# Shift and scale of the first norm: from split to plain fp32 products in two column tiles of TensorE

## Chip, cores and metric

One core of a Trainium2 chip runs one layer of a backbone on 256 latent and 256 context tokens of width 2048, in fp32. The metric is the device time of one execution in microseconds.

## The reference, cut to what matters

For the latent tokens and for the context tokens (with `c_ctx` in place of `c`) the layer begins with

```python
mod = silu(c) @ ada_w + ada_b          # (2048) @ (2048, 12288): six sections of 2048 columns
h   = rmsnorm(x) * (1 + scale1) + shift1   # section 0 is the shift, section 1 the scale
z   = h @ w_in                         # (2048, 3680)
```

Attention, spatial gating, a gated linear attention, an output projection and a mixture of 16 experts follow. Of `ada_w`, sections 0 and 1 (2 x 16.8 MB) are needed before the first projection; the other four belong to later places.

## The kernel before, in words

**Stages.** `phase1` computes the first norm and the in-projection. Behind it come the mixers, the output projection, the second norm, routing, and the expert stage, which streams 403 MB of weights.

**The first norm.** `rows` loads x and ctx (8 loads of 512 KB on SP) and takes their sums of squares on ACT; `scale` multiplies the rows. `ada1(f0, nf)` makes shift and scale for `nf` blocks ("columns") of 128 model dimensions from block `f0` on, for both token kinds at once. The units are (0, 2), (2, 2), (4, 4), (8, 4), (12, 4). A unit has three parts: `load` steps, `copies` and `cols`, and one `hcol` for each column.

- `load(sec, k0)` brings 4 blocks of 128 rows of `ada_w` for one section into a `raw` buffer (pool of 6, shared with the loads of `w_in`), in 512 KB loads by SP (L169). A unit of two columns is loaded in pieces of 1 KB, one of four in pieces of 2 KB. ACT rounds the buffer to fp32r (`hi`, L129), DVE forms the rest (`lo`, L130), each in a pool of two buffers. TensorE multiplies both (L347) with a weight tile of four columns (`c4`: the rounded value and the rest of silu(c) and of silu(c_ctx)). Only section 0 of the first unit goes unsplit, as plain fp32 products (L342).
- `copies` brings the sums from PSUM to SBUF on ACT (L356). `cols` transposes them on TensorE (L365) and adds the parts and the bias on DVE (L368 to L372).
- `hcol(j)` transposes one column of x and ctx (4 transposes into a `psB` bank, L384, two such banks), applies scale and shift on ACT (L388, two halves), and splits the result into `hT` (L129 on ACT, L130 on DVE).

**The in-projection.** `w_in_steps(k0, k1, chunk)` streams `w_in` by chunks of columns: a load into `raw`, the split (three buffers each), and three fp32r products (L425) for each 128 tokens and 128 rows. `hT` has four quarters of four columns. In a first round all nine chunks are multiplied with the first quarter alone (`win`, k 0 to 4), woven with the later units of `ada1`; when the norm is complete, a second round (`w1`, `w2`, `w3`) takes quarters two to four and adds.

**What sets the order.** Program order, woven by `merge` and `weave`, is the priority by which a scheduler orders each engine's instructions ahead of time; every engine then works strictly in that order. SP issues nearly all loads, so a load that waits for its buffer holds all loads behind it.

```python
units = [self.ada1(*u) for u in ((0, 2), (2, 2), (4, 4), (8, 4), (12, 4))]
...
for l, p, h in units[2:]:
    rest += merge(l, late) + p
    late = h
weave(win[1:], rest + late)
```

Of the kernel before, what the change touches and what calls it, by code (L numbers as in the profile page):

```python
# [18 lines left out]
D = 2048  # L19
KT = 16  # L20
# [4 lines left out]
KQ = KT // NQ  # L25
# [73 lines left out]
class Kern:  # L99
# [112 lines left out]
    def phase1(self):  # L212
        nc, tc, T = self.nc, self.tc, self.T
# [8 lines left out]
        with ExitStack() as ph, ExitStack() as p1:  # L222
# [4 lines left out]
            self.adap = [p1.enter_context(self.pool(name=n, bufs=2, side="right")) for n in ("ahi", "alo")]  # L227
# [40 lines left out]
            self.c4 = self.cp.tile([128, KT, 2, 2], F32R, name="c4")  # L268
            scv = self.sc.rearrange("p (v k) -> p k v", v=2)
            nc.scalar.activation(self.c4[:, :, :, 0], scv, AF.Copy)  # L270
            nc.vector.tensor_tensor(self.c4[:, :, :, 1], scv, self.c4[:, :, :, 0], op=OP.subtract)
# [21 lines left out]
            units = [self.ada1(*u) for u in ((0, 2), (2, 2), (4, 4), (8, 4), (12, 4))]  # L293
# [3 lines left out]
            win = [f for c in chunks for f in self.w_in_steps(0, 4, c)]  # L297
            for f in [rows(i) for i in range(4)] + l0[:2] + [scale(0)] + l0[2:] + p0 + h0 + win[:1] + l1 + p1_ + h1 + [scale(1)]:
                f()
# [21 lines left out]
    def ada1(self, f0, nf):  # L321

        nc = self.nc
        T = self.T
        st = {}
        cw = nf * 128
        q, j0 = divmod(f0, KQ)

        whole = (f0 == 0, False)
        rows = [2 if w else 4 for w in whole]  # L330
        scv = self.sc.rearrange("p (v k) -> p k v", v=2)

        def load(sec, k0):
            def f():
                if k0 == 0:
                    st[sec] = self.C()
                c0 = sec * D + f0 * 128
                if whole[sec]:
                    raw = self.rawp.tile([128, 4, cw], F32, name="raw", tag="raw")
                    nc.sync.dma_start(raw, T["ada_w"][0, k0 * 128:(k0 + 4) * 128, c0:c0 + cw].rearrange("(k p) c -> p k c", p=128))  # L340
                    for k in range(4):
                        nc.tensor.matmul(st[sec][:2, :cw], scv[:, k0 + k], raw[:, k], start=(k0 + k == 0), stop=(k0 + k == KT - 1))  # L342
                    return
                h, l = self.stream(T["ada_w"][0], c0, c0 + cw, k0, 4, self.adap)
                for part, w in enumerate((h, l)):
                    for k in range(4):
                        nc.tensor.matmul(st[sec][:4, :cw], self.c4[:, k0 + k].rearrange("p a b -> p (a b)"),  # L347
                                         w[k], start=(k0 + k == 0 and part == 0),
                                         stop=(k0 + k == KT - 1 and part == 1))
            return f  # L350

        def copies():
            s4 = self.maccp.tile([128, 1024], F32, name="macc", tag="macc")
            st["s4"] = [s4[:rows[i], i * cw:(i + 1) * cw] for i in range(2)]
            for sec in range(2):
                nc.scalar.activation(st["s4"][sec], st[sec][:rows[sec], :cw], AF.Copy)  # L356

        def cols():
            cps = self.B()
            md = self.sp.tile([128, 2, KQ, 2], F32, name="md", bufs=2)[:, :, :nf]  # L360
            for sec in range(2):
                n = rows[sec]
                for j in range(nf):
                    o = sec * 16 + j * n
                    nc.tensor.transpose(cps[:, o:o + n], st["s4"][sec][:, j * 128:(j + 1) * 128], self.ident[:n, :n])  # L365
                cv = cps[:, sec * 16:sec * 16 + nf * n].rearrange("p (k v a) -> p k v a", k=nf, v=2)
                b = self.col[:, 48 + 16 * sec + f0:48 + 16 * sec + f0 + nf]
                nc.vector.tensor_tensor(md[:, sec], cv[:, :, :, 0], b[:, :, None].to_broadcast([128, nf, 2]), op=OP.add)  # L368
                if not whole[sec]:
                    nc.vector.tensor_tensor(md[:, sec], md[:, sec], cv[:, :, :, 1], op=OP.add)  # L370
# [4 lines left out]
            if j0 == 0:  # L375
                h = self.h_new(q)
                self.hT[q] = (h[:, 0], h[:, 1])

        def hcol(j):
            def f():  # L380
                k = f0 + j
                tp = self.B()
# [3 lines left out]
                md = st["md"]  # L386
# [4 lines left out]
                self.split(hi[:, j0 + j], lo[:, j0 + j], full)  # L391
            return f
        out = []
# [1191 lines left out]
```

## Time and profile before

| | |
|---|---|
| three runs | 1649.9, 1656.56, 1658.26 us (median 1656.56) |
| the profiled execution | 1650.78 us, span 1649.0 us |
| TensorE products (PE) | busy 1487.6 us, 90% of the span |
| VectorE (DVE), ScalarE (ACT) | 647.5 us (39%), 447.6 us (27%) |
| HBM read | 566.73 MB, 346 GB/s over the span |

The profile is of one execution. Its span is read as stages: from about 740 us on the expert stage moves 420 to 422 GB/s in nearly every slice. The change lies in the first 165 us, where PE, DVE, ACT and DMA all have high shares, so only a view of that stretch tells what sets its time. A busy share of PE counts modelled ends, which overlap the next start; two starts give the true spacing.

### The profile page before, as it was taken

To read this page: it belongs to the slowest core of one execution; us is meant where nothing else is said; L and a number is where in the kernel's file an instruction comes from. 1 tells how busy PE (TensorE), PEld (TensorE's weight loads), DVE (VectorE), ACT (ScalarE), POOL (GpSimd) and SP (SyncE) were. 2 spreads that over 40 slices of the span, in tenths; PEclk is the share of its full clock that TensorE was granted. 3 is DMA by queue.
4 is the path that set the end of the run, shared out by engine and by line. 5 is a ranking of instruction groups with operands and counts; after the bars stand their busy time and mean duration, and the time that the engine had idled before them with its cause. 6 is when DMAs were issued, how large, how long until landed. Compare 5 with 4: busy or idle time off the path is not lost. (4 is left out here: it accounts for less than half of the span.)

```text
span 1649.0 us, 17919 instructions
## 1 busy us (share of the span) xinstructions
PE 1487.6 (90%) x6875; PEld 793.5 (48%) x6875; DVE 647.5 (39%) x1093; ACT 447.6 (27%) x870; POOL 37.7 (2%) x52
## 2 busy tenths in 40 slices
PE   4999999998899989899998988997988998988877
PEld 1566878986667758443333333333333333333322
DVE  4687788988987665311111121111021111111102
ACT  4788224257656543210011001011001001001000
POOL 0000100001000000000000000000000000000000
PEclk9999999999999999899999999999999999999999
DMA  9899987765787577689999999999999999999996
GB/s 296 262 322 318 324 284 235 239 228 159 248 290 248 195 231 305 243 324 422 421 420 421 421 420 421 421 421 421 421 420 421 419 421 421 420 421 420 422 421 243
DMA packets 140880, 570.09 MB, mean 346 GB/s; under 512 B 19195, under 2 KB 37906, under 8 KB 92662
## 3 DMA queue, kind: packets, MB, share of 16 engines
q1 hardware_dynamic: 133424, 563.93, 88.0%
q0 software_dynamic: 1696, 2.97, 0.6%
q10 hardware_dynamic: 5670, 1.99, 0.5%
q8 instruction: 56, 0.92, 0.2%
q14 instruction: 34, 0.28, 0.1%
HBM read 566.73 MB, written 4.21 MB: 346 GB/s over the span
## 5 line engine op out<-in xcount | busy, mean ns | idle before, releaser
L1295 PE MATMUL psC<-mraw,xT 128*64 128x512 f32 x2048 | 466.1, 595 | 66.0 <-DMA mraw<-in_moe_w_dram 66.0
L1295 PEld LDWEIGHTS psC<-mraw,xT 128*64 128x64 f32 x2048 | 154.6, 137 | 372.2 <-issue 245.9
L1295 PE MATMUL psA<-mraw,aT 128*64 128x512 f32 x1024 | 225.8, 597 | 0.0
L130 DVE TENSOR_TENSOR lo<-raw,hi 128x1024 fp32r<-128x1024 f32 (+3 forms) x170 | 198.3, 1182 | 64.0 <-ACT hi L129 56.6
L1385 DVE TENSOR_TENSOR act<-silu,psC 64x512 f32<-64x512 f32 x32 | 22.0, 690 | 488.5 <-ACT silu L1296 488.5
L129 ACT ACTIVATE hi<-raw 128x1024 fp32r<-128x1024 f32 (+3 forms) x170 | 171.3, 1024 | 155.9 <-DMA raw<-in_w_in_dram 57.6
L1296 ACT ACTIVATE silu<-psC 64x512 f32<-64x512 f32 x32 | 18.9, 590 | 701.0 <-PE psC L1295 701.0
L425 PE MATMUL psA<-hi,hT 128*128 128x512 f32 (+2 forms) x832 | 182.2, 346 | 5.6 <-ACT hi L129 2.3
L425 PEld LDWEIGHTS psA<-hi,hT 128*128 128x128 f32 x832 | 136.3, 190 | 28.1 <-ACT hi L129 5.8
L1295 PEld LDWEIGHTS psA<-mraw,aT 128*64 128x64 f32 x1024 | 74.2, 138 | 138.3 <-issue 134.8
L1401 DVE TENSOR_TENSOR zs<-psA,gate 128x512 f32<-128x512 f32 x64 | 44.3, 692 | 173.7 <-PE psA L1295 171.9
L425 PE MATMUL psA<-lo,hT 128*128 128x512 f32 (+2 forms) x416 | 106.0, 348 | 0.9 <-DVE lo L130 0.9
L1295 PE MATMUL psB<-Sr,x 128*128 128x256 f32 x256 | 70.6, 412 | 22.8 <-ACT xT L1296 20.9
L455 DVE SCALAR_TENSOR_TENSOR gate<-raw,sc,gate 128x1024 f32<-128x1024 f32 x64 | 81.9, 1280 | 3.9 <-DMA raw<-in_ada_w_dram 3.7
L455 DVE SCALAR_TENSOR_TENSOR macc<-raw,sc,macc 128x1024 f32<-128x1024 f32 x60 | 76.7, 1279 | 14.9 <-DMA raw<-in_ada_w_dram 14.4
L425 PEld LDWEIGHTS psA<-lo,hT 128*128 128x128 f32 x416 | 70.2, 190 | 11.1 <-issue 1.5
L1295 PEld LDWEIGHTS psB<-Sr,x 128*128 128x128 f32 x256 | 47.8, 201 | 50.3 <-ACT xT L1296 34.2
L1295 PE MATMUL psB<-zs,W 128*128 128x512 f32 x128 | 62.8, 619 | 1.7 <-DVE stage L1437 1.5
L1437 DVE TENSOR_TENSOR stage<-stage,psB 128x512 f32<-128x512 f32 x64 | 43.3, 686 | 45.5 <-PE psB L1295 44.9
L1296 ACT ACTIVATE xT<-psB,mod 128x256 f32<-128x256 f32 x64 | 36.0, 563 | 78.0 <-PE psB L1295 78.0
L347 PE MATMUL psC<-hi,c 128*4 128x512 f32 (+1 forms) x144 | 36.9, 361 | 13.4 <-ACT hi L129 12.8
L1295 PEld LDWEIGHTS psB<-zs,W 128*128 128x128 f32 x128 | 21.1, 189 | 39.1 <-DVE stage L1437 20.1
(389 smaller groups left out, 1333.9 us busy)
## 6 DMA issues: line engine op xcount, KB each, us to landing
mraw<-in_moe_w_dram SPq DMA_DIRECT2D x383, 1024.0 KB, 19.8
raw<-in_ada_w_dram SPq DMA_DIRECT2D x192, 512.0 KB, 5.0
raw<-in_w_in_dram SPq DMA_DIRECT2D x44, 512.0 KB, 5.1
raw<-in_w_out_dram SPq DMA_DIRECT2D x32, 512.0 KB, 4.7
raw<-in_w_in_dram SPq DMA_DIRECT2D x10, 432.0 KB, 5.2
raw<-in_mla_w_ukv_dram SPq DMA_DIRECT2D x8, 512.0 KB, 5.0
raw<-in_mla_w_uq_dram SPq DMA_DIRECT2D x8, 384.0 KB
xs<-in_x_dram SPq DMA_DIRECT2D x4, 512.0 KB, 4.7
```

Of the source, the lines that this page charges most:

```text
L129: self.nc.scalar.activation(hi, src, AF.Copy)
L130: self.nc.vector.tensor_tensor(lo, src, hi, op=OP.subtract)
L347: nc.tensor.matmul(st[sec][:4, :cw], self.c4[:, k0 + k].rearrange("p a b -> p (a b)"), w[k], start=(k0 + k == 0 and part == 0), stop=(k0 + ...
L425: nc.tensor.matmul(acc[t][:, :w], xw[:, j, t * 128:(t + 1) * 128], ww[:, k], start=(kk == k0 and p == 0 and k == 0), stop=(kk + n == k1 an ...
L455: i = nc.vector.scalar_tensor_tensor(a, raw, self.sc[:, k:k + 1], a, op0=OP.mult, op1=OP.add)
L1295: mm = lambda *a, **kw: tc.keep_in_program_order(nc.tensor.matmul(*a, skip_group_check=True, **kw))
L1296: act_op = lambda *a, **kw: tc.keep_in_program_order(nc.scalar.activation(*a, **kw))
L1385: TT(a[:, h * 512:(h + 1) * 512], s, st["U"][h][CAP:], op=OP.mult)
L1401: TT(st["zs"][:, s], st["Z"][j], self.gate2[:, s], op=OP.mult)
L1437: TT(s, s, p, op=OP.add)
```

## The change

`ada1` no longer splits its weights. Every product is a plain fp32 one, with a weight tile of two columns (silu(c) and silu(c_ctx)); two products stand in two column tiles of TensorE, with output partitions from 0 and from 64. In units of two and four columns the tiles hold the two sections. The last two units become one, (8, 8), which loads 128 rows of 1024 columns at a time, in pieces of 4 KB, and has two PSUM banks, one for each section, and in each the two halves in the two tiles. A `load` step now brings both sections (two loads of 512 KB) into a pool of its own, `araw`, with four buffers. The products of a step are chained, so that the tiles alternate. `c4` is gone, and `cols` has half as many rows to transpose and no parts to add. The eight `hcol` of the last unit all come behind its products. In the changed code the in-projection's line is L424, the products' L347, the loads' L339, the transposes' L368 and L386, and `hcol`'s on ACT L390.

```diff
-            self.adap = [p1.enter_context(self.pool(name=n, bufs=2, side="right")) for n in ("ahi", "alo")]
+            self.adap = p1.enter_context(self.pool(name="araw", bufs=4, side="right"))
...
-            units = [self.ada1(*u) for u in ((0, 2), (2, 2), (4, 4), (8, 4), (12, 4))]
+            units = [self.ada1(*u) for u in ((0, 2), (2, 2), (4, 4), (8, 8))]
...
-        cw = nf * 128
+        cw = min(nf * 128, 512)
+        nb = nf * 128 // cw
+        per = 1024 // (cw * nb)
...
+        place = lambda sec, b: (sec, 64 * b) if nb == 2 else (0, 64 * sec)
...
-                h, l = self.stream(T["ada_w"][0], c0, c0 + cw, k0, 4, self.adap)
-                for part, w in enumerate((h, l)):
-                    for k in range(4):
-                        nc.tensor.matmul(st[sec][:4, :cw], self.c4[:, k0 + k].rearrange("p a b -> p (a b)"),
-                                         w[k], start=(k0 + k == 0 and part == 0),
-                                         stop=(k0 + k == KT - 1 and part == 1))
+                for sec in (1, 0):
+                    raw = self.adap.tile([128, per, nb * cw], F32, name="araw", tag="araw")
+                    c0 = sec * D + f0 * 128
+                    self.last_load = nc.sync.dma_start(raw, T["ada_w"][0, k0 * 128:(k0 + per) * 128, c0:c0 + nb * cw].rearrange("(k p) c -> p k c", p=128))
+                    raws.append((sec, raw))
+                todo = [(k, sec, b, raw) for k in range(per) for sec, raw in raws[::-1] for b in range(nb)]
+                last = None
+                for k, sec, b, raw in todo:
+                    i, o = place(sec, b)
+                    with self.tc.high_priority(), self.tc.issue_after(last.ins) if last else nullcontext():
+                        last = nc.tensor.matmul(st["ps"][i][o:o + 2, :cw], scv[:, k0 + k], raw[:, k, b * cw:(b + 1) * cw],
+                                                start=(k0 + k == 0), stop=(k0 + k == KT - 1), skip_group_check=True)
...
-        for k0 in range(0, KT, 4):
-            out += [load(1, k0), load(0, k0)]
-        return out, [copies, cols], [hcol(j) for j in range(nf)]
+        return [load(k0) for k0 in range(0, KT, per)], [copies, cols], [hcol(j) for j in range(nf)]
```

Three places of the new order. First SP's loads, from the third unit to the end of shift and scale. Before:

```order
L169 DMA raw<-in_ada_w_dram 128x2x512 x4
L169 DMA raw<-in_w_in_dram 128x2x512
L169 DMA raw<-in_ada_w_dram 128x2x512 x2
L169 DMA raw<-in_w_in_dram 128x2x512
L169 DMA raw<-in_ada_w_dram 128x2x512 x4
L169 DMA raw<-in_w_in_dram 128x2x512
L169 DMA raw<-in_ada_w_dram 128x2x512 x2
```

and now:

```order
L339 DMA araw<-in_ada_w_dram 128x2x512 x8
L169 DMA raw<-in_w_in_dram 128x288
L339 DMA araw<-in_ada_w_dram 128x2x512 x6
L169 DMA raw<-in_w_in_dram 128x2x512
L339 DMA araw<-in_ada_w_dram 128x2x512 x2
L169 DMA raw<-in_w_in_dram 128x2x512 x2
L339 DMA araw<-in_ada_w_dram 128x1024 x32
L169 DMA raw<-in_w_in_dram 128x2x512 x3
```

The `w_in` loads of this stretch moved ahead of the large unit, whose 32 loads follow one another.

Second, TensorE's products in the middle of the large units. Before (`c` is the split weight tile, two records of `hi` and `lo` for each load half):

```order
L347 MATMUL psC<-hi,c_157 4x512 x4
L347 MATMUL psC<-lo,c_157 4x512 x4
L347 MATMUL psC<-hi,c_157 4x512 x2
L425 MATMUL psA<-hi,hT_287 128x288 x2
L425 MATMUL psA<-lo,hT_287 128x288
L347 MATMUL psC<-hi,c_157 4x512 x2
L347 MATMUL psC<-lo,c_157 4x512 x2
```

and now:

```order
L347 MATMUL psC<-araw,sc 2x512 x4
L424 MATMUL psA<-hi,hT_247 128x288 x2
L424 MATMUL psA<-lo,hT_247 128x288 x3
L424 MATMUL psA<-hi,hT_247 128x288 x5
L347 MATMUL psC<-araw,sc 2x512 x4
L424 MATMUL psA<-hi,hT_247 128x288
L424 MATMUL psA<-lo,hT_247 128x288 x3
L424 MATMUL psA<-hi,hT_247 128x288 x6
```

A step is now four products in a row, with in-projection products between any two steps.

Third, TensorE behind the last product of shift and scale, now (`ident` marks transposes, `hT_247` is the first quarter, `hT_644` the second):

```order
L347 MATMUL psC<-araw,sc 2x512 x4
L424 MATMUL psA<-hi,hT_247 128x512 x2
L424 MATMUL psA<-lo,hT_247 128x512 x2
L368 MATMUL psB<-ident,araw 128x2 x8
L386 MATMUL psB<-ident,xs_123 128x128 x3
L368 MATMUL psB<-ident,araw 128x2 x8
L386 MATMUL psB<-ident,xs_123 128x128 x5
L424 MATMUL psA<-hi,hT_247 128x512 x5
...
L386 MATMUL psB<-ident,xs_123 128x128 x16
L424 MATMUL psA<-hi,hT_247 128x512 x6
...
L386 MATMUL psB<-ident,xs_123 128x128 x4
L424 MATMUL psA<-hi,hT_644 128x288 x6
```

Before, 16 transposes of x and ctx stood behind the last product, four at a time between in-projection products; now 32 do, 16 of them in one run.

## Rows read from the trace of the kernel before

**Rows 1.** The windows of the first 200 us, 20 us each. Columns: stretch; its length; busy us of PE, PEld, DVE, ACT and POOL, with the number of instructions behind each; granted TensorE clock (1.00 is full); mean busy share of the 16 DMA engines; GB/s moved.

```profile
0.00:20.00 20.00, 1.01 (x4) 0.67 (x4) 1.77 (x12) 10.30 (x18) 3.29 (x9) 1.00 0.82 269
20.00:40.00 20.00, 17.21 (x87) 6.58 (x88) 14.68 (x24) 9.27 (x14) 0.00 (x0) 1.00 0.99 321
40.00:60.00 20.00, 18.27 (x103) 10.12 (x102) 14.98 (x20) 14.49 (x19) 0.00 (x0) 1.00 0.84 268
...
140.00:160.00 20.00, 19.52 (x91) 11.73 (x89) 16.03 (x18) 17.31 (x24) 0.00 (x0) 1.00 1.02 342
160.00:180.00 20.00, 20.00 (x146) 19.14 (x146) 12.80 (x16) 9.26 (x17) 4.00 (x6) 1.00 0.89 306
180.00:200.00 20.00, 17.80 (x82) 14.74 (x81) 16.51 (x21) 3.32 (x4) 2.75 (x4) 0.91 0.93 326
```

**Rows 2.** The waits of 0 to 165 us, two rows of TensorE. Columns: engine, tile and line that waited, for whom; us in total, times, longest us.

```profile
PEld psC L347 <- ACT hi L129: 20.9, 20, 11.4
PE psC L347 <- ACT hi L129: 12.8, 6, 11.3
```

**Rows 3.** The waits of SP's own queue, same stretch and columns.

```profile
SPq L169 <- DVE lo L130: 72.3, 58, 3.8
```

**Rows 4.** TensorE's timeline in two places, the large units of the shift and scale and the in-projection behind them. Columns: start us, us to the modelled end of the last one, engine, line, operation, out<-in, weight tile, moving tile, count. What one costs is the difference of two starts over the count.

```profile
131.07 1.08 PE L425 MATMUL psA<-hi,hT 128*128 128x512 f32 x4
132.00 0.40 PE L425 MATMUL psA<-lo,hT 128*128 128x512 f32 x1
132.34 0.63 PE L347 MATMUL psC<-hi,c 128*4 128x512 f32 x2
...
170.27 0.96 PE L425 MATMUL psA<-hi,hT 128*128 128x288 f32 x6
171.06 0.56 PE L425 MATMUL psA<-lo,hT 128*128 128x288 f32 x3
```

**Rows 5.** TensorE's timeline at three moments: the last product of the second unit, the last product of shift and scale, and the first in-projection product that uses the second quarter of the norm.

```profile
53.60 0.63 PE L347 MATMUL psC<-lo,c 128*4 128x256 f32 x4 [0.35 <-DVE lo L130]
...
154.03 1.09 PE L347 MATMUL psC<-lo,c 128*4 128x512 f32 x4
...
163.87 0.96 PE L425 MATMUL psA<-hi,hT 128*128 128x288 f32 x6
```

**Rows 6.** Groups by line and shape, 0 to 200 us. Columns: line, engine, operation, out<-in, shapes, count | busy us, mean ns of one | idle time before them and what ended it.

```profile
L130 DVE TENSOR_TENSOR lo<-raw,hi 128x1024 fp32r<-128x1024 f32 x75 | 89.9, 1223 | 30.0 <-ACT hi L129 22.9 <-issue 3.1 <-ACT zcB L432 3.0
L129 ACT ACTIVATE hi<-raw 128x1024 fp32r<-128x1024 f32 x75 | 77.2, 1055 | 43.2 <-DMA raw<-in_w_in_dram 10.1 <-PE psC L347 9.3 <-DMA wg<-in_gla_wg_f_dram 9.2
...
L347 PE MATMUL psC<-lo,c 128*4 128x512 f32 x96 | 29.0, 397 | 0.2 <-DVE lo L130 0.2
...
L388 ACT ACTIVATE hfull<-psB,md 128x256 f32<-128x256 f32 x32 | 16.3, 563 | 2.0 <-DVE md L372 2.0
...
L129 ACT ACTIVATE hT<-hfull 128x512 fp32r<-128x512 f32 x16 | 10.1, 632 | 0.0
...
L356 ACT ACTIVATE macc<-psC 4x512 f32<-4x512 f32 x6 | 3.4, 573 | 0.0
```

**Rows 7.** TensorE's timeline in the expert stage: full fp32 products (weight tile 128\*128), transposes, and fp32 products in two column tiles (weight tile 128\*64). One fp32 product has two records.

```profile
781.80 7.03 PE L1295 MATMUL psB<-x,G 128*128 128x512 f32 x16
788.67 4.03 PE L1295 MATMUL psB<-zs,W 128*128 128x512 f32 x8
...
793.62 0.46 PE L1393 MATMUL psB<-ident,act 64*128 64x64 f32 x4 [0.47 <-ACT aT L1296]
794.01 6.23 PE L1295 MATMUL psA<-mraw,aT 128*64 128x512 f32 x28
...
1222.98 3.65 PE L1295 MATMUL psC<-mraw,xT 128*64 128x512 f32 x16 [0.93 <-DMA mraw<-in_moe_w_dram]
```

**Rows 8.** DMA issues of the 512 KB loads of `ada_w`: of the whole execution, of 0 to 200 us, and of 30.4 to 32 us. Columns: out<-in, queue, operation, count, KB each, median us from issue to landing.

```profile
raw<-in_ada_w_dram SPq DMA_DIRECT2D x192, 512.0 KB, 5.0
...
raw<-in_ada_w_dram SPq DMA_DIRECT2D x83, 512.0 KB, 6.0
...
raw<-in_ada_w_dram SPq DMA_DIRECT2D x2, 512.0 KB, 3.6
```

**Rows 9.** ACT's timeline, splits of loads and one column of the norm (`hfull`, then its rounding `hT`). Columns as in rows 4.

```profile
132.70 3.90 ACT L129 ACTIVATE hi<-raw 128x1024 fp32r<-128x1024 f32 x4
...
162.08 1.47 ACT L388 ACTIVATE hfull<-psB,md 128x256 f32<-128x256 f32 x3
163.42 0.64 ACT L129 ACTIVATE hT<-hfull 128x512 fp32r<-128x512 f32 x1
```

**Rows 10.** TensorE's timeline where it waited at 183 us.

```profile
185.71 1.17 PE L425 MATMUL psA<-hi,hT 128*128 128x512 f32 x4 [2.20 <-DVE zxR L434]
...
187.35 1.91 PE L425 MATMUL psA<-hi,hT 128*128 128x512 f32 x4
189.05 1.06 PE L425 MATMUL psA<-lo,hT 128*128 128x512 f32 x2
189.91 1.33 PE L425 MATMUL psA<-hi,hT 128*128 128x512 f32 x4
```

**Rows 11.** One window of the expert stage, columns as in rows 1.

```profile
800.00:820.00 20.00, 20.00 (x96) 6.75 (x94) 2.77 (x4) 0.00 (x0) 0.00 (x0) 1.00 1.01 420
```

More of the change, by code (lines that the diff above doesn't have):

```diff
@@ L267, in phase1 @@
             nc.vector.tensor_tensor(self.sc, e, self.col[:, 0:32], op=OP.mult)
[L268 to L271, printed above, removed]
             self.hT = {}
@@ L297, in phase1 @@
             win = [f for c in chunks for f in self.w_in_steps(0, 4, c)]
-            for f in [rows(i) for i in range(4)] + l0[:2] + [scale(0)] + l0[2:] + p0 + h0 + win[:1] + l1 + p1_ + h1 + [scale(1)]:
+            for f in [rows(i) for i in range(4)] + l0[:1] + [scale(0)] + l0[1:] + p0 + h0 + win[:1] + l1 + p1_ + h1 + [scale(1)]:
                 f()
@@ L325, in ada1, with load @@
         st = {}
-        cw = nf * 128
-        q, j0 = divmod(f0, KQ)
-        whole = (f0 == 0, False)
-        rows = [2 if w else 4 for w in whole]
+        cw = min(nf * 128, 512)
+        nb = nf * 128 // cw
+        per = 1024 // (cw * nb)
         scv = self.sc.rearrange("p (v k) -> p k v", v=2)
-        def load(sec, k0):
+        place = lambda sec, b: (sec, 64 * b) if nb == 2 else (0, 64 * sec)
+        def load(k0):
             def f():
                 if k0 == 0:
[L336 to L340, printed above, removed]
-                    for k in range(4):
-                        nc.tensor.matmul(st[sec][:2, :cw], scv[:, k0 + k], raw[:, k], start=(k0 + k == 0), stop=(k0 + k == KT - 1))
-                    return
-                h, l = self.stream(T["ada_w"][0], c0, c0 + cw, k0, 4, self.adap)
-                for part, w in enumerate((h, l)):
-                    for k in range(4):
-                        nc.tensor.matmul(st[sec][:4, :cw], self.c4[:, k0 + k].rearrange("p a b -> p (a b)"),
-                                         w[k], start=(k0 + k == 0 and part == 0),
-                                         stop=(k0 + k == KT - 1 and part == 1))
@@ new lines, in f @@
+                    st["ps"] = [self.C() for _ in range(nb)]
+                raws = []
+                for sec in (1, 0):
[4 more added lines that the diff above has]
+                todo = [(k, sec, b, raw) for k in range(per) for sec, raw in raws[::-1] for b in range(nb)]
@@ L354, in copies @@
-            st["s4"] = [s4[:rows[i], i * cw:(i + 1) * cw] for i in range(2)]
+            st["s2"] = {}
             for sec in range(2):
-                nc.scalar.activation(st["s4"][sec], st[sec][:rows[sec], :cw], AF.Copy)
+                if sec == 0 or nb == 2:
+                    s2 = self.adap.tile([128, 1024], F32, name="araw", tag="araw")[:2].rearrange("p (i c) -> p i c", i=2)
+                for b in range(nb):
+                    i, o = place(sec, b)
+                    st["s2"][sec, b] = s2[:, b if nb == 2 else sec, :cw]
+                    nc.scalar.activation(st["s2"][sec, b], st["ps"][i][o:o + 2, :cw], AF.Copy)
@@ L358, in cols @@
         def cols():
             cps = self.B()
-            md = self.sp.tile([128, 2, KQ, 2], F32, name="md", bufs=2)[:, :, :nf]
+            md = self.sp.tile([128, 2, 8, 2], F32, name="md", bufs=2)[:, :, :nf]
             for sec in range(2):
-                n = rows[sec]
                 for j in range(nf):
-                    o = sec * 16 + j * n
-                    nc.tensor.transpose(cps[:, o:o + n], st["s4"][sec][:, j * 128:(j + 1) * 128], self.ident[:n, :n])
-                cv = cps[:, sec * 16:sec * 16 + nf * n].rearrange("p (k v a) -> p k v a", k=nf, v=2)
+                    c = sec * 16 + j * 2
+                    b, jj = divmod(j * 128, cw)
+                    nc.tensor.transpose(cps[:, c:c + 2], st["s2"][sec, b][:, jj:jj + 128], self.ident[:2, :2])
+                cv = cps[:, sec * 16:sec * 16 + nf * 2].rearrange("p (k v) -> p k v", v=2)
@@ L381, in f @@
                 k = f0 + j
+                q, kq = divmod(k, KQ)
+                if kq == 0:
+                    h = self.h_new(q)
+                    self.hT[q] = (h[:, 0], h[:, 1])
                 tp = self.B()
@@ L390, in f @@
                 hi, lo = self.hT[q]
-                self.split(hi[:, j0 + j], lo[:, j0 + j], full)
+                self.split(hi[:, kq], lo[:, kq], full)
             return f
-        out = []
-        for k0 in range(0, KT, 4):
-            out += [load(1, k0), load(0, k0)]
-        return out, [copies, cols], [hcol(j) for j in range(nf)]
+        return [load(k0) for k0 in range(0, KT, per)], [copies, cols], [hcol(j) for j in range(nf)]
     CH = [[([(2368, 2624), (3648, 3680)], ("zxR", ZK), ("zcB", CK)), ([(2624, 3136)], ("zxB", ZL), ("zcB", CL)),
```

8 lines of the change are left out of this document (1 added, 7 removed).

## The prediction

> **What bounds the kernel now.** I read the windows of the first 200 us first, because the diff touches nothing later, then the waits, then single stretches of the timeline. The windows [rows 1] show three stages. Up to about 40 us the DMA engines are full (share 0.99 at only 321 GB/s: the pieces are 1 KB) and TensorE waits. From 40 to 60 us DMA share falls to 0.84 and TensorE is still not full. By 140 us TensorE is busy 19.5 of 20 us, with DMA share at 1.02 and 342 GB/s: both are near their limit. "Busy" flatters TensorE, since modelled ends overlap, so I took start-to-start times [rows 4]: four fp32r records of 512 columns take 0.93 us (0.233 each) and six of 288 columns 0.79 us (0.1325), that is 0.46 ns per column, and they follow each other without a gap. There the order of the PE program is what sets the time.
>
> The waits confirm it. TensorE waits 33.7 us for ACT's rounded copy, but 11.4 and 11.3 of these (PEld and PE, the same gap) are the first product at 21.8 us [rows 2]; the rest is small pieces. The long entry is on SP: its loads wait 72.3 us in 58 pieces for DVE to release a raw buffer [rows 3]. This is the best argument for the change, and it says that loads are late, not that TensorE is.
>
> Three moments fix the stage [rows 5]: the second unit's last product ends at 54.2 us, the last product of shift and scale ends at 155.0 (154.03 + 0.93 by spacing), and the first in-projection product that uses the second quarter of the norm starts at 163.87. Behind that moment all five engines have the same instruction order before and after, apart from two neighbours changing places on DVE and ACT, so the change is worth what it moves that moment by, as long as the stages behind pass a shift on.
>
> **The splits removed.** 60 of the loads lose their split: 60 x 1.055 us on ACT (63 us) and 60 x 1.223 us on DVE (73 us) [rows 6]. I cost this at nothing: both run beside TensorE and DMA, which set the time behind the second unit. Without that cover it would be worth at most ACT's part.
>
> **The products.** Per 512 columns of both sections the old form takes four fp32r records, 4 x 0.233 = 0.93 us. The new form takes four fp32 records in two column tiles. The expert stage has just this shape: a burst of 16 records lasts 3.65 us [rows 7], which with a last record of 0.59 us means two records start every 0.427 us; alone on the full array 16 records take 6.87 us, 0.43 each. So 0.853 us for the four, and a step of the large unit (eight records) 1.71 us instead of 1.85. Over the 48 pairs of 512 columns that is 3.6 us less TensorE work, over the first unit's unsplit section, now in a tile beside the other, another 3.4: 7 us at most, where TensorE is the limit.
>
> **The path, step by step, for the changed order.**
> (a) To 54 us. Needed until the second unit's last product: x and ctx 4.2 MB, two units 8.4 MB, the w_in loads that SP now issues between them 2.7 MB: 15.4 MB with the small ones. By 40 us 11.8 MB are in (20 us at 269 and at 321 GB/s); 3.6 MB more at 0.32 MB/us end at 51, and the last group's products bring 54. Unchanged.
> (b) 54 to 61 us. The order puts no product of the third unit ahead of the second unit's columns, as it did before, so TensorE waits for two copies, the transposes and two columns on ACT (four half columns at 0.45 us and two roundings at 0.52 [rows 9]): about 4 us; 12 in-projection products, 2.8 us, follow. 61.
> (c) Third unit, 8 steps of 1.71, between them 16 products of 512, 48 of 288 and 24 of 256 columns (3.7 + 6.4 + 2.9 = 13.0 us): 26.7 us, to 87.7. Its columns, 20 products and the transposes: 6.3 us, to 94.0.
> (d) The large unit, 16 steps. TensorE needs 1.71 + 1.4 us a step (93 products of 288, 32 of 512 and 12 transposes in 15 gaps, 21 us). But four buffers hold two steps: a step's two loads are issued when the step two before it is done. They land after some 5.0 us (page median of the 512 KB loads; 3.6 the shortest shown, 6.0 the median of the first 200 us [rows 8]; I take the middle, as the queue holds little but the next pair). The period is then (5.0 + 1.71) / 2 = 3.36 us, more than 3.11: 15 x 3.36 + 1.71 = 52.1, to 146.1. The old last product was at 155.0: 9 us won here.
> (e) The tail. Before, four columns were left at this point; now all eight of the large unit are, in one run. ACT has 4 copies (0.57 each [rows 6]), 4 splits (0.98), 8 columns of 2 x 0.45 + 0.52 and two evictions before TensorE's last in-projection product of the first quarter; with two psB buffers a column's transposes wait for the column two before it. I step this: copies done 2.3 us after the last product, first column from 3.5, fourth done at 10, the next split at 11, then 24 products (5.6) and two columns' transposes (0.8): 17.5. TensorE's own work there is 40 products and 48 transposes, 14.1 us, so it idles some 3.4. Such idling has a second price: after a wait of 2.2 us at 183 us six products took 2.56 us instead of 1.39 [rows 10], so 1.2 us more. Tail 18.7 against 8.9 (163.87 - 155.0).
> Sum: 146.1 + 18.7 = 164.8 against 163.87, **+0.9 us**. What (d) wins, (e) gives back.
>
> The stretch behind passes it on: DMA share is 0.89 and 0.93 in the next two windows [rows 1], so loads could swallow a gain of some us there, and the expert stage, at DMA share 1.01 [rows 11], is as long as its bytes. The profiled execution took 1650.78 us; with +0.9 it is 1651.7. The median of the three runs lies 5.8 us above that execution, so I say **1657 us**.
>
> **Bounds.** The landing time of (d): at 3.6 us TensorE is the limit (-3.7), at 6.0 the period is 3.86 (+7.5, and +2.1 in (c)). A change of tile shape: between the stretches of full and tiled products the trace shows 0.34 us instead of 0.23 once [rows 4] and 0.39 us for four transposes of 0.1 before tiled products [rows 7], so 0 to 0.1 us; 54 such changes cost 0 to 5.9 us, and I take 0, since the old order changes shape about as often. (a) could be 2 us shorter at 342 GB/s.
>
> **Rivals.**
> 1. *Loads were the limit, and they are free now.* The 72 us of SP's waits speak for it, TensorE's dense records [rows 4] against it. Then (d) runs at TensorE's pace (-3.7), (a) wins 2, ACT without splits does (b) 3 us sooner, and the tail is TensorE's work alone (-4.6): -13.3 + 0.9 = -12.4, 1645 us.
> 2. *The four buffers become the wait* (slower). Buffers were free some 2.3 us after landing (1.055 + 1.223 on ACT and DVE); now TensorE holds each until its in-order turn, and two steps of lookahead must cover issue and landing. It decides from a landing of 2 x 3.11 - 1.71 = 4.5 us; at the 6.0 us that the first 200 us show it costs 7.5 + 2.1, so 0.9 + 9.6 = +10.5, 1667 us. Against it: those 6.0 us were measured with up to six loads queued.
> 3. *Each change of tile shape waits for the array to empty* (slower). A 512-column record lasts 0.40 us [rows 6] and the next starts after 0.233, so emptying would cost 0.17 us; 54 times 9.2, 1667 us. Rows 7 show 0.39 us for four transposes and the change, which leaves next to nothing. The Trainium skill, TensorEngine Tiling (Array Packing), section Tiling Modes, says that changing the tiling mode drains the engine; by that rule this rival would hold, and the trace as far as it shows one does not agree.
> 4. *The two tiles do not run side by side* (the change does not do what it says). Then 192 records of 512 and 128 of 256 columns cost twice: 192 x 0.2135 + 128 x 0.107 = 55 us, less 4 us hidden behind loads: 1708 us. The bursts in rows 7 speak against it.
>
> **How the numbers follow.** Forecast 0.5, own range 1651 to 1664. Rival 1: 0.25. Rival 2: 0.17. Rival 3: 0.06. Rival 4: 0.02. The range reaches from below rival 1 to above rival 2, 1643 to 1669. About 0.5% (8 us) is what a measurement of this kernel can tell from no change; by the cases faster is 0.25, the same 0.5, slower 0.25.
>
> **What would show it.** In the profile of the changed kernel: the bursts of four products at L347 in 1.6 to 1.9 us; the last of them near 146 us; TensorE waiting for DMA of the new tile in the large unit, some 0.25 us a step, and for ACT behind the last product; the first product on the second quarter at 165 us; the rest the same. Wrong would be a last product after 152 us with DMA waits above 0.5 us a step (rival 2) or gaps that no wait explains at each change of shape (rival 3), a first second-quarter product before 156 us (rival 1), or bursts of 3.4 us (rival 4).

## The result and the profile after

The changed kernel takes **1662.11 us** (median of 11 runs, 1658.89 to 1666.93), the kernel before 1653.45 (11 runs): ratio **1.0056**, 95% interval 1.004 to 1.0072. It is slower by some 9 us. The forecast was +0.9 us, 1657, range 1643 to 1669. The profiled execution took 1660.39 us, span 1658.6: 9.6 us over the one before.

Windows of the changed kernel, columns as in [rows 1]:

```profile
0.00:20.00 20.00, 1.01 (x4) 0.67 (x4) 2.25 (x16) 10.78 (x20) 3.30 (x9) 1.00 0.84 278
20.00:40.00 20.00, 14.25 (x76) 4.98 (x76) 9.71 (x16) 5.13 (x8) 0.00 (x0) 0.83 0.98 317
40.00:60.00 20.00, 15.71 (x100) 8.13 (x100) 2.33 (x6) 4.14 (x10) 0.00 (x0) 0.99 0.92 301
60.00:80.00 20.00, 19.16 (x78) 10.14 (x79) 2.61 (x3) 5.21 (x9) 0.00 (x0) 0.84 0.65 219
80.00:100.00 20.00, 19.85 (x113) 11.56 (x112) 4.47 (x7) 7.50 (x14) 0.00 (x0) 1.00 0.85 290
120.00:140.00 20.00, 20.00 (x105) 9.53 (x103) 4.13 (x4) 4.89 (x10) 0.00 (x0) 1.00 0.88 305
160.00:180.00 20.00, 18.09 (x113) 15.80 (x113) 14.56 (x17) 17.44 (x32) 3.02 (x5) 1.00 0.65 202
```

Against [rows 1], the loss is early: from 20 to 60 us TensorE is busy 30.0 us where it was 35.5, its granted clock is 0.83 of full from 20 to 40 us and 0.84 from 60 to 80, and in the latter window the DMA engines are two thirds full. DVE and ACT have lost their splits, and the kernel is slower all the same.

TensorE's timeline of the changed kernel, the same moments as [rows 5] and what lies between (columns as in rows 4):

```profile
30.16 6.42 PE L347 MATMUL psC<-araw,sc 128*2 128x256 f32 x32 [3.48 <-DMA araw<-in_ada_w_dram]
...
54.94 1.90 PE L347 MATMUL psC<-araw,sc 128*2 128x256 f32 x16 [2.29 <-DMA araw<-in_ada_w_dram]
...
60.84 4.21 PE L424 MATMUL psA<-hi,hT 128*128 128x512 f32 x9 [1.63 <-ACT hT L129]
64.85 1.05 PE L424 MATMUL psA<-lo,hT 128*128 128x512 f32 x2
65.70 0.63 PE L424 MATMUL psA<-hi,hT 128*128 128x512 f32 x1
66.26 2.03 PE L347 MATMUL psC<-araw,sc 128*2 128x512 f32 x8
...
102.19 1.89 PE L347 MATMUL psC<-araw,sc 128*2 128x512 f32 x8
...
104.89 0.69 PE L424 MATMUL psA<-hi,hT 128*128 128x288 f32 x4
105.51 1.89 PE L347 MATMUL psC<-araw,sc 128*2 128x512 f32 x8
107.33 0.54 PE L424 MATMUL psA<-hi,hT 128*128 128x288 f32 x2
...
153.49 1.89 PE L347 MATMUL psC<-araw,sc 128*2 128x512 f32 x8
155.30 0.74 PE L424 MATMUL psA<-hi,hT 128*128 128x512 f32 x2
...
163.58 0.66 PE L386 MATMUL psB<-ident,xs 128*128 128x128 f32 x4 [0.85 <-ACT hfull L390]
165.01 0.65 PE L386 MATMUL psB<-ident,xs 128*128 128x128 f32 x4 [0.77 <-ACT hfull L390]
165.95 1.66 PE L424 MATMUL psA<-hi,hT 128*128 128x512 f32 x6 [0.29 <-ACT hi L129]
...
172.44 1.03 PE L424 MATMUL psA<-hi,hT 128*128 128x288 f32 x6
```

The reader sees TensorE waiting for DMA at 26.7 and 52.7 us, then nine products of 512 columns in 4.01 us, 0.446 each, nearly twice the 0.233 of [rows 4]. The third unit begins at 66.26 us, 11.7 us later than before (54.55). The last product of shift and scale ends at 155.30, as before; the second quarter begins at 172.44 instead of 163.87, **8.6 us later**, and from there the two programs have one order.

The granted clock at those places, in windows of 2 us of the changed kernel, columns as in rows 1:

```profile
28.00:30.00 2.00, 0.00 (x0) 0.00 (x0) 0.46 (x1) 0.00 (x0) 0.00 (x0) 0.76 1.09 359
30.00:32.00 2.00, 1.83 (x10) 0.62 (x12) 0.00 (x0) 0.00 (x0) 0.00 (x0) 0.50 1.09 343
62.00:64.00 2.00, 2.00 (x7) 1.52 (x6) 0.63 (x1) 0.00 (x0) 0.00 (x0) 0.50 0.48 177
64.00:66.00 2.00, 2.00 (x6) 1.31 (x4) 0.00 (x0) 0.06 (x1) 0.00 (x0) 0.50 0.00 0
```

TensorE's waits for the new loads in the changed kernel (who waited for whom; us, times, longest us):

```profile
PE psC L347 <- DMA araw<-in_ada_w_dram: 15.8, 3, 10.0
```

And the waits of SP's own queue there, 0 to 175 us, same columns:

```profile
SPq L339 <- PE psC L347: 64.8, 39, 6.6
SPq L169 <- DVE lo L130: 13.6, 6, 3.8
```

0.50 is the lower of the clock's two levels, 1.2 GHz. Of the 15.8 us, 10.0 are the wait for the very first product, which the kernel before has too (11.3 us [rows 2]). SP's wait of [rows 3] has not gone: it waited 72.3 us for DVE, and now waits 64.8 us for TensorE's own products to release the new buffers (plus 13.6 for DVE). At 64 to 66 us not a byte moves: the four buffers are full and TensorE works at half speed through products that come first in its order.

### The profile page after: what moved, and what is told of

It is laid out like the page before. It is cut to its first block, busy times and chain, and to the rows that moved or that the text cites. A ratio compares the mean times of both kernels' runs of the same rounds, so it can differ in the third digit from the quotient of the medians.

```text
span 1658.6 us, 17690 instructions
## 1 busy us (share of the span) xinstructions
PE 1491.4 (90%) x6875; PEld 785.1 (47%) x6875; DVE 577.4 (35%) x1020; ACT 391.1 (24%) x809; POOL 37.5 (2%) x52
## 5 line engine op out<-in xcount | busy, mean ns | idle before, releaser
L424 PE MATMUL psA<-hi,hT 128*128 128x512 f32 (+2 forms) x832 | 187.6, 351 | 9.1 <-DVE zxR L433 3.4
L130 DVE TENSOR_TENSOR lo<-raw,hi 128x1024 fp32r<-128x1024 f32 (+3 forms) x110 | 126.8, 1159 | 104.8 <-ACT hi L129 81.7
L424 PEld LDWEIGHTS psA<-hi,hT 128*128 128x128 f32 x832 | 137.1, 192 | 41.2 <-issue 17.4
L129 ACT ACTIVATE hi<-raw 128x1024 fp32r<-128x1024 f32 (+3 forms) x110 | 110.6, 1011 | 183.9 <-DMA raw<-in_w_in_dram 79.0
L424 PE MATMUL psA<-lo,hT 128*128 128x512 f32 (+2 forms) x416 | 107.0, 350 | 0.9 <-DVE lo L130 0.9
L347 PE MATMUL psC<-araw,sc 128*2 128x512 f32 (+1 forms) x320 | 65.5, 547 | 16.0 <-DMA araw<-in_ada_w_dram 15.8
L424 PEld LDWEIGHTS psA<-lo,hT 128*128 128x128 f32 x416 | 70.2, 190 | 18.2 <-issue 9.3
L1436 DVE TENSOR_TENSOR stage<-stage,psB 128x512 f32<-128x512 f32 x64 | 43.3, 686 | 45.8 <-PE psB L1294 44.9
```

The lines of the kernel that those rows point to most:

```text
L129: self.nc.scalar.activation(hi, src, AF.Copy)
L130: self.nc.vector.tensor_tensor(lo, src, hi, op=OP.subtract)
L347: last = nc.tensor.matmul(st["ps"][i][o:o + 2, :cw], scv[:, k0 + k], raw[:, k, b * cw:(b + 1) * cw], start=(k0 + k == 0), stop=(k0 + k == ...
L424: nc.tensor.matmul(acc[t][:, :w], xw[:, j, t * 128:(t + 1) * 128], ww[:, k], start=(kk == k0 and p == 0 and k == 0), stop=(kk + n == k1 an ...
L1436: TT(s, s, p, op=OP.add)
```

## The experiments

Three theories for the 9 us. **Buffers**: the old loads had a pool of six, shared with the loads of `w_in` and released by DVE; the new ones have four, released by TensorE in its turn, and `copies` puts its sums into buffers of the same four. **Tail**: eight columns in one run behind the last product. **Clock and order**: TensorE's idle pieces up to 66 us, and half speed behind them. All ratios below are to the kernel before, run on the same chip.

**One: the large unit cut again.**

```diff
-units = [... (4, 4), (8, 8)]
+units = [... (4, 4), (8, 4), (12, 4)]
```

> The changed kernel with its large unit (8 columns) cut into two units of 4 columns, each with 2 KB pieces and with its own copies and columns; the products stay plain fp32 in two column tiles. Changed kernel for comparison: last product 155.30 us, first product on the second quarter 172.44 us, tail between them 17.1 us; kernel before: 155.0, 163.87, tail 8.9. Theory TAIL (the eight columns that all come behind the last product are what costs): tail back to 9 to 10 us, first second-quarter product at 164 to 167 us, time 6 to 8 us below the changed kernel. Theory EARLY (TensorE's idle gaps up to 66 us and the halved clock behind them cost the 9 us): the front is unchanged, so work that leaves the tail only fills the middle; last product near 162 us, first second-quarter product at 170 us or later, time within 3 us of the changed kernel. Theory SHAPE (fp32 bursts with their changes of shape take as long as the old fp32r products): neither; the time goes by the other two.

Measured: 1657.5 us, 1.0037 (1.0019 to 1.0056): 4.6 us off the changed kernel's median, between the two expectations; by the ratios it is 0.2% or 3 us, and the intervals overlap (1.004 to 1.0072 for the changed kernel). The first product on the second quarter starts at 161.39 us, sooner than either theory said: in this order it stands ahead of the last product of shift and scale (which ends at 168.7 us), so that moment can't be compared. TensorE's 1.6 us of waits for `hfull` are gone, and the last 288-column products of the second round's first chunk start at 186.7 instead of 191.2. Of those 4.4 us, 1.8 were already there at the third unit's first product (64.48), up to which both programs are the same: one front varies by that much between two executions.

**Two: more buffers.** Shift loads from the six-buffer pool, scale loads from the four:

```diff
-raw = self.adap.tile(...)
+raw = self.adap.tile(...) if sec else self.rawp.tile(...)
```

> The changed kernel with the shift section's loads taken from the six-buffer pool that the in-projection's weights use, and only the scale section's from the four buffers: up to four load steps ahead instead of two. Changed kernel: second unit's last product at 56.84 us, third unit's first at 66.26, last product of all at 155.30, first second-quarter product 172.44. Rival 2 (the four buffers are the wait): the second unit ends by 54 us, the third unit's products meet no late load, first second-quarter product 4 to 6 us sooner, 166 to 168, time 3 to 6 us lower. Theory EARLY in the form that the order and the clock cost, and not the buffers: second unit's end moves by under 2 us, the gap from 57 to 66 us stays, time within 2 us. The large unit shows no DMA wait in the changed kernel, so no theory expects a gain there; the shared pool may make in-projection weights late instead, which would show as DMA waits on the 288-column products.

Measured: **1649.9 us**, 1.0005 (0.999 to 1.0021). The loss is gone, and the second quarter moves by twice what the expectation gave. Second unit's last product at 45.8 us, third unit's first at 45.65, second quarter at 159.52: 12.9 us sooner than in the changed kernel and 4.4 sooner than before. (Of these 4.4 us the ratio shows at most 1.7, by the lower end of its interval: the moment and the time agree only roughly.) Its windows, columns as in rows 1:

```profile
20.00:40.00 20.00, 16.89 (x114) 7.04 (x115) 8.46 (x15) 4.77 (x9) 0.00 (x0) 1.00 1.09 351
40.00:60.00 20.00, 19.16 (x98) 8.51 (x97) 3.09 (x6) 5.08 (x9) 0.00 (x0) 1.00 1.02 362
60.00:80.00 20.00, 20.00 (x106) 10.69 (x105) 2.74 (x3) 5.63 (x10) 0.00 (x0) 1.00 0.88 303
```

351 and 362 GB/s against 317 and 301, and the granted clock is 1.00 in all three: TensorE's idling, the low clock and the idle DMA went together.

But the line changed two things. With the shift loads in the pool of `w_in`, the order of SP's loads is another one as well. SP's queue up to the second unit's last loads, some of its rows (start us, us, queue, line, operation, out<-in, count), first of the changed kernel:

```profile
15.56 2.69 SPq L169 DMA_DIRECT2D raw<-in_w_in_dram  x2
...
27.68 2.77 SPq L169 DMA_DIRECT2D raw<-in_w_in_dram  x5
...
38.65 0.51 SPq L169 DMA_DIRECT2D raw<-in_w_in_dram  x1
44.18 4.34 SPq L339 DMA_DIRECT2D araw<-in_ada_w_dram  x4
```

and of run two:

```profile
22.01 1.42 SPq L169 DMA_DIRECT2D raw<-in_w_in_dram  x1
...
34.18 2.60 SPq L339 DMA_DIRECT2D raw<-in_ada_w_dram  x2
```

Eight loads of `w_in` (2.7 MB) stand ahead of the second unit's last load in the changed kernel, one (0.5 MB) in run two, and one in the kernel before. From 20 us until the second unit's last product starts, the changed kernel moved 11.0 MB at 303 GB/s, run two 9.1 MB at 356. At run two's rate the 11.0 MB would have taken 31 us instead of 36.5; so, as an estimate, half of the 11 us that this product comes sooner is the rate, and the other half is bytes that no longer stand ahead of it. No run keeps SP's order and changes the buffers alone.

The tail, from the last product (142.34) to 159.52, is still 17.2 us, but almost without waits, and the loss is gone all the same. So its length is no loss; it is in-projection work that comes later.

**Three: order.**

```diff
-... + win[:1] + l1 + p1_ + h1 + [scale(1)]
+... + win[:1] + l1 + l2[:2] + p1_ + h1 + [scale(1)]
```

> The changed kernel with the first two load steps of the third unit (16 products) put ahead of the second unit's columns in the order, as the kernel before had products of the next unit there. Changed kernel: second unit's last product 56.84 us, third unit's first 66.26, TensorE idle 58.9 to 60.84 for ACT and at 1.2 GHz from 60 to 66 us. Theory EARLY: the third unit's first products start at 57 to 59 us, the idle piece for ACT is filled, the clock stays at 2.4 GHz there, first second-quarter product 3 to 5 us sooner, time 3 to 5 us lower. Theory TAIL: nothing of the tail is touched; it stays 17 us and the time falls only by the few us that the front gains. Rival: the loads of these steps are not there yet, because the four buffers are freed only by the second unit's products; then TensorE waits for DMA of the new tile at 57 to 60 us and the columns come later, time within 1.5 us or higher.

Measured: 1665.4 us, 1.0084 (1.0059 to 1.0108), the slowest of the runs that keep the pairs; the rival held. With four buffers the third unit's loads can't be issued before the second unit's products are done, and now the columns wait behind them, at half clock too (0.50 from 60 to 68 us). TensorE's timeline of this run, a row of eight products that lasts 3.58 us:

```profile
60.88 3.58 PE L348 MATMUL psC<-araw,sc 128*2 128x512 f32 x8 [4.94 <-DMA araw<-in_ada_w_dram]
```

**Four: the clock.** Small products in the idle gaps, after the steps named:

```diff
+for _ in range({(0, 4): 14, (2, 8): 10}.get((f0, k0), 0)):
+    matmul(st["ps"][0][32:34, :128], scv[:, 0], self.ident)   # 8 more behind k == 3's transposes
```

> The changed kernel with 32 small fp32 products added whose results go to a corner of a bank that nothing reads: 14 behind the second load step of the first of the new units, 10 behind the third step of the second, 8 behind the transposes of the fourth column. They run in TensorE's idle gaps (27 to 30, 53 to 55, 59 to 61 us) and move no data sooner. Theory CLOCK: the granted clock stays at 2.4 GHz at 30 to 36 and at 60 to 66 us; the nine 512-column products of 60.84 us take 2.1 us instead of 4.0, first second-quarter product 3 to 5 us sooner, time 3 to 5 us lower. If the loads set the early pace and not the clock: the second unit's end stays within 1 us of 56.84 whatever the clock, and only the 2 us behind 60.84 are won. If the halved clock costs nothing (work behind it waits for loads anyway): time within 1 us, or higher by the 32 products, at most 32 x 0.1 = 3 us.

Measured: 1662.4 us, 1.0072 (1.005 to 1.0095): no gain. At 60 to 66 us the clock did stay at 2.4 GHz, and at 30 to 36 us too, but at 36 to 46 us it fell instead, as two windows of this run show (columns as in rows 1):

```profile
36.00:46.00 10.00, 8.04 (x35) 4.31 (x36) 2.84 (x6) 3.77 (x9) 0.00 (x0) 0.66 0.74 247
...
60.00:66.00 6.00, 6.00 (x30) 3.14 (x29) 1.38 (x2) 2.29 (x5) 0.00 (x0) 1.00 0.51 190
```

The third unit begins 2.4 us sooner (63.84), but 1.31 us go to a wait for `araw` at 87 us, and the last product of shift and scale is 0.9 us sooner. In this execution, taking the second low stretch away brought no more than that, and one front varies by up to 1.8 us between two executions. The first low stretch only moved, so what it costs by itself isn't settled.

**Five and six: where the buffers bite.** Run two's line with a condition on the unit:

```diff
+raw = self.adap.tile(...) if sec or f0 >= 4 else self.rawp.tile(...)    # five; f0 < 4 in six
```

> The changed kernel with the shift section's loads taken from the six-buffer pool in the first two units alone (columns 0 to 3); the third and the large unit keep the four buffers for both sections. With six buffers for the shift in all units the first second-quarter product came at 159.5 us instead of 172.4 and the time fell by 12 us. Theory EARLY BUFFERS (the four buffers bite only while loads are the limit, up to 66 us): all of it is kept, second unit's last product by 46 us instead of 56.84, time within 2 us of the run with six buffers in all units, 10 us or more below the changed kernel. Rival, lookahead in the third and large unit matters too: half or less of the 12 us.

> The converse: six buffers for the shift section in the third and the large unit, the four buffers for both sections in the first two. Theory EARLY BUFFERS: second unit's last product stays at 56 to 57 us, the large unit has no DMA wait to lose; only the third unit's loads can be issued ahead, which takes away part of the gap from 57 to 66 us: 0 to 5 us below the changed kernel, time above 1656. Rival: 8 us or more below it, if the gap before the third unit's first product is what counts and not the first two units.

Measured: five 1653.6 us, 0.9989 (0.997 to 1.0007); six 1656.3, 1.0024 (1.0004 to 1.0044). First second-quarter product 166.41 and 166.10 us, against 172.44 with neither and 159.52 with both: 6.0 and 6.3 us, and together 12.9. At that point my theory (early only) falls. The times don't say so: by the ratios run five keeps all of run two's gain (0.9989 against 1.0005, intervals overlapping), and they are too close to share the gain out. Nor are the two halves clean, since SP's order moves in both. In run five one load of `w_in` is left ahead of the second unit's last load. In run six two are, with four shift loads of the third unit; the second unit ends at 58.08 us, and the third begins before that, at 44.70. Why the later units need the buffers, though the changed kernel has no DMA wait in its large unit, run five shows (TensorE's timeline, the end of its large unit):

```profile
132.75 1.89 PE L347 MATMUL psC<-araw,sc 128*2 128x512 f32 x8 [0.37 <-DMA araw<-in_ada_w_dram]
135.69 1.89 PE L347 MATMUL psC<-araw,sc 128*2 128x512 f32 x8 [1.05 <-DMA araw<-in_ada_w_dram]
139.88 2.82 PE L347 MATMUL psC<-araw,sc 128*2 128x512 f32 x8 [2.31 <-DMA araw<-in_ada_w_dram]
142.63 2.34 PE L424 MATMUL psA<-hi,hT 128*128 128x512 f32 x6
```

Once the front is early, TensorE catches up with the loads, waits up to 2.31 us and runs at half speed again (six products in 2.17 us, to the next start at 144.80). In the changed kernel, with its later front, no such wait shows.

**Seven: buffers and cut**, runs one and two together.

> Six buffers for the shift section in all units, and the large unit cut in two units of four columns. Alone, the buffers gave 12 us and the cut 4.6 us (1649.9 and 1657.5 against 1662.1). If the two are independent (front and tail): 1645 us, 7 us below the kernel before. If the time won at the front is taken back behind, by waits for the in-projection's buffers or for the splits: 1649 to 1652.

Measured: 1650.6 us, 0.9985 (0.9964 to 1.0005). With buffers there, the cut gives nothing that the runs can tell.

**Eight: no pairing.** Units of four, each section in its own bank at the same tile:

```diff
-place = lambda sec, b: (sec, 64 * b) if nb == 2 else (0, 64 * sec)
+place = lambda sec, b: (sec, 0)
```

> The changed kernel with units of four columns, each section in a bank of its own at the same column tile, so that no two products stand side by side. Where pairing works, a product of 512 columns costs 0.213 us in a pair and 0.43 alone: 192 of 512 and 128 of 256 columns add some 50 us, first second-quarter product near 215 us, time 1700 to 1710. If pairs gain little (the two tiles share what limits them): under 1680. Each visit of fp32 products in the changed kernel takes about 0.2 us more than its records' spacing, at entry and exit together; if that comes from the tile shape (2 columns in the upper or lower half), it stays; if it came from two tiles being in flight at once, it falls below 0.1.

Measured: 1704.3 us (one run), the second quarter at 215.53, both as expected. TensorE's timeline of this run, eight products from start to the next start, with the two before them:

```profile
102.57 0.42 PE L424 MATMUL psA<-lo,hT 128*128 128x288 f32 x2
102.92 3.60 PE L347 MATMUL psC<-araw,sc 128*2 128x512 f32 x8
106.45 0.40 PE L424 MATMUL psA<-lo,hT 128*128 128x288 f32 x1
```

3.53 us where the pairs take 1.82. Pairing works. The two products ahead take 0.35 us instead of 0.265, so the price of entry is there without two tiles in flight.

Does every change of shape cost this? The kernel before goes between 128\*128 and 128\*4 products of fp32r just as often; its timeline, into such products and out of them:

```profile
112.02 0.56 PE L425 MATMUL psA<-lo,hT 128*128 128x288 f32 x3
112.42 1.08 PE L347 MATMUL psC<-hi,c 128*4 128x512 f32 x4
...
114.26 0.62 PE L347 MATMUL psC<-hi,c 128*4 128x512 f32 x2
114.72 0.43 PE L425 MATMUL psA<-hi,hT 128*128 128x288 f32 x2
```

Three products of 288 columns take 0.40 us up to the change, 0.133 each, and two of 512 take 0.46 before the change back, 0.23 each: the spacing that they have among their own kind. So a narrow weight tile alone doesn't cost it. Nor does plain fp32 alone: seven fp32 transposes on the full array in front of a visit take 0.86 us in run eleven (94.05 to 94.91), where 0.109 each would be 0.76. The price is that of going into the 128\*2 fp32 products and out of them.

**Nine to eleven, and a last one: orders on top of the buffers.** Nine is two and three together, ten adds the cut. In eleven, on top of two, two load steps are put into one; the last run is eleven with the first such pair ahead of the second unit's columns.

```diff
+loads = [pair(a, b) for a, b in zip(loads[::2], loads[1::2])]     # nf >= 4
```

> Six buffers for the shift section in all units, and the first two load steps of the third unit put ahead of the second unit's columns. With the buffers alone the first second-quarter product came at 159.52 us and the time was 1649.9; with the order alone the time rose to 1665, because TensorE waited 4.9 us for those loads, with four buffers. Theory: the order costs only where the loads can't be issued ahead; with six buffers they can, TensorE has no wait for DMA of the new tiles at 45 to 52 us, first second-quarter product at 157 to 159.5, time 0 to 3 us below 1649.9. Rival: the loads are the limit at 50 us whatever the buffers, so the columns come later and nothing is gained: 160 us or later, time the same or higher.

> Six buffers, the order and the cut of the large unit into two of four columns together. The cut beside the buffers gave no measurable gain (1650.6 against 1649.9), as TensorE was dense behind the last product anyway. Expected: as with buffers and order alone, within 2 us; 1647 to 1651. If the order removes the front's last gap and the cut the splits' waits behind: 1645 or less.

> Six buffers as in the second run, and two load steps of the third and large unit put side by side in the order: half as many visits of fp32 products (12 instead of 24), each of 16 products. Theory SHAPE (a visit of eight products takes 1.82 us plus some 0.2 at its two changes of shape): 12 visits fewer save 12 x 0.2 = 2.4 us where TensorE is dense, first second-quarter product near 157 us instead of 159.5. If the 0.2 us are not of the change of shape but of each product group: no difference. Against both: a visit needs four buffers at once, so loads may come late; then DMA waits show in the large unit and it is slower.

> Six buffers, two load steps of the third and large unit side by side, and the first such pair ahead of the second unit's columns. The six buffers with the pairs took 1646.8 us (0.997 of the kernel before), but the planner split the pairs up again in most places: 21 visits of fp32 products behind the second unit instead of 24, and only three of them with 16 products. So if the changes of shape were what it won, 3 x 0.2 us would be all; the rest is the order in which the loads are issued. Theory: with the pair ahead of the columns TensorE has no wait at 50 us, and the time is 1645 to 1648. Rival: within the spread of the runs with six buffers, 1648 to 1650, which would say that none of the orders is worth more than 0.2%.

Measured: nine 1649.2 us, 0.9982 (0.9961 to 1.0003); ten **1647.8**, 0.9969 (0.995 to 0.9987); eleven **1646.8**, 0.997 (0.9952 to 0.9987); the last 1649.5, 0.9983 (0.9964 to 1.0002). Ten and eleven beat both kernels, the one before by 0.3%. Among the runs with six buffers in all units they hardly stand out: run two's interval begins at 0.999 where theirs end at 0.9987, all others overlap, and in the last run the rival held. Run eleven split most pairs up again; where one stayed whole its timeline gives the price of a product inside a visit (the rows left out are 12 more of the same products):

```profile
97.31 1.03 PE L347 MATMUL psC<-raw,sc 128*2 128x512 f32 x4
...
100.84 1.66 PE L428 MATMUL psA<-hi,hT 128*128 128x512 f32 x6
```

16 products in 3.53 us, against 1.82 for eight: 1.71 for each eight more, and 0.11 for leaving.

## Why the forecast missed by 8 us

The range held, the sign of the likeliest case did not: +0.9 forecast, about +9 measured. At the first second-quarter product it is 172.44 against 164.8, 7.6 us, which the steps make up as +2.8, +2.4, +2.9, +1.0 and -1.6.

- **(a) 54 us, "unchanged": 56.84. This is the step that failed.** I counted bytes and took [rows 1]'s 320 GB/s as the rate, and I counted four buffers only in the large unit. But with four buffers SP waits for TensorE's products from the first unit on. The 2.7 MB of `w_in` in my sum were right, but I took them as fixed. Run two has the moment at 45.8 us, at a higher rate (356 GB/s against 303 from 20 us on) and with 2.2 MB of `w_in` fewer ahead; by the estimate under run two each is worth about half.
- **(b) 7 us to the third unit: 9.4.** The wait and the columns were right in kind; the products behind them ran at 1.2 GHz after TensorE had idled 2.29 and 1.63 us. I had priced such idling in the tail [rows 10], and not here.
- **(c) 33 us: 35.9, and the product's price.** Inside a visit a step costs 1.71 us, as forecast. But the four products before a visit take 0.62 us instead of 0.53 (104.89 to 105.51), and leaving costs 0.11: 0.2 us a visit. I took 0 from a bound of 0 to 0.1 per change; the upper end was right. My reason for 0, that the old order changes shape about as often, fails: the old changes cost nothing (run eight). The 0.34 us of [rows 4] was a single case, and the 0.39 us of [rows 7] comes from transposes that stand in a tile of 64 rows (64\*128) themselves. A step is then 1.91 us instead of the old 1.85: **the change saves TensorE nothing in the large units**, 24 x 0.06 = 1.4 us the other way. Eight visits explain 1.6 of the 2.9 us here; the rest is not traced.
- **(d) 52.1 us: 53.1, for another reason.** Not loads (no DMA wait in this unit) but TensorE's own work with 0.2 us more a step set it (51.3 us for 15 steps, 3.42 each, where I had 3.11). That this lies beside my load period of 3.36 is luck. Loads set the pace only behind an earlier front, as at the end of run five's large unit.
- **(e) 18.7 us: 17.1.** Right in size; TensorE idled 1.9 us there (0.85, 0.77 and 0.29), not 3.4. But "what (d) wins, (e) gives back" suggested a price for the eight columns; runs two and seven show that a long tail without waits costs nothing.
- **Rival 1** (1645): it needed loads that are free, and they weren't. Given more buffers the kernel comes nearer to it, but not there: 0.997 to 1.0005 of the kernel before, where 1645 of 1657 is 0.993.
- **Rival 2** (1667, chance 0.17) is what happened: the four buffers became the wait. Its total, +10.5, is close; its place was wrong. I put it in the third and the large unit; by the second quarter's start in runs five and six about half of it sits in the first two, where I had left the loads unchanged.
- **Rival 3** (0.17 us a change): 0.1 measured, one of the reasons for step (c), and only for the changes into and out of the 128\*2 fp32 products; 0.2 us for both changes of a visit, where emptying the array would by my working be 0.34. The Trainium skill, TensorEngine Tiling (Array Packing), section Tiling Modes, says that a change of tiling mode drains the engine. The traces agree in kind, with a smaller price than I had worked out; whether the 128\*4 products, which pay nothing, are a change of mode at all, they don't show.
- **Rival 4** is out: run eight shows what it would have cost, some 47 us over run one, which has the same units.

Shown by runs: that the loss hangs on the pool of the shift loads (two, five, six), that putting the third unit ahead makes it worse while there are four buffers (three), that pairing works (eight). Read from traces only: the price of the changes of shape. Open: how much of the pool's effect is the number of buffers and how much the order of SP's loads that comes with it, how much of run one's gain is the tail, and what the low clock at 30 to 36 us costs by itself.

## What to carry to other kernels

When a change removes a stage between a load and its product, ask who frees the buffer now and how many loads that lets run ahead, from the first load on and not only where the stream is longest; bytes over bandwidth is a bound only as long as buffers are free. Look also at what another pool does to the order of the loads, since that decides which bytes stand ahead. A cheaper product is priced per visit, with the change of shape on both sides, not per column (here 0.2 us a visit, which used up the gain of eight products). A wait that a trace doesn't show may be hidden by an earlier delay, and returns when that delay is mended.

## What the chip showed that was not expected

The price of 0.2 us for going from full fp32r products to fp32 products with a 128\*2 weight tile and back is nearly the same with pairs (0.09 before, 0.11 behind) and without (0.085 and some 0.1), while going to 128\*4 fp32r products and back cost nothing. And the rate of loads in 1 KB pieces was not at its limit with DMA share 0.99 and 321 GB/s [rows 1]. That is a mean with dips in it: in windows of 2 us the kernel before has share 1.09 and 348 GB/s at 20 to 22 us, and 0.63 and 208 at 26 to 28. With more buffers the same pieces came at 351 GB/s, share 1.09, over the whole 20 us.
